# SwiGLU in a two-layer hybrid encoder trunk: gate and up products by rows, on a transposed x whose norm factor is applied behind the product

## The chip, the core and the metric

The kernel runs on one core of one Trainium2 chip. The metric is the device time of one execution in microseconds (us), lower is better. Engines: PE (TensorE, matmuls; PEld is its weight load), DVE (VectorE), ACT (ScalarE), POOL (GpSimd) and SP (SyncE, which here issues the DMAs).

## The reference

Two layers over x of 256 tokens by 1024 channels, float32. Each layer has a mixer (three groups of dilated-window attention beside a Hyena long convolution, merged by gates) and a SwiGLU, each between two RMSNorms. What the change touches is the second line of a layer's end:

```python
x = x + rms_norm(m, norm_mix_post[l])
u = rms_norm(x, norm_ffn_pre[l])                     # x * rsqrt(mean(x*x) + 1e-6) * gain
a, b = jnp.split(u @ w_gu, 2, axis=-1)               # w_gu: 1024 x 5632
x = x + rms_norm((jax.nn.silu(a) * b) @ w_down, norm_ffn_post[l])
```

## The kernel before

**Arithmetic.** A weight comes from memory as a "piece", one tile of 128 partitions by 1024 (or 768) float32. ACT rounds it to `whi` (L86, `hi_of`) and DVE, or for every fifth piece POOL, takes the rest `wlo` (L89, `lo_of`). Activations are split the same way (`UH`/`UL`). `mm3` (L80) then makes three matmuls, high by high, high by low, low by high, in place of one. All have L78 in the profile.

**Two forms of product.** `col_proj` (L409) keeps a 128x128 block of weights stationary and streams all 256 tokens, so that one piece gives 128 output channels in transposed form: 24 matmuls of 256 columns. `rows_of`/`rows` (L420, L424) keep a 128x128 block of the transposed activations stationary and stream the weights, 384 or 512 columns wide, once for each of the two tiles of 128 tokens: 12 matmuls for a piece, and the result has tokens on the partitions.

**Pieces.** `order()` (L116) lists the pieces. `split_hi` and `split_lo` take the next one; `piece()` (L171) keeps three ready ahead of the one it hands out. Raw tiles have four buffers, so SP issues the next load when an earlier raw tile has been split.

**SwiGLU before.** `ffn` (L802) takes the first 384 channels of gate and of up by rows (eight pieces of 768 columns, in `start`), multiplies SiLU(gate) by up there, and transposes the three blocks with six PE transposes (`first`, L810). The other 19 blocks are pairs of `col_proj` calls (L825), whose product (L828) is already transposed. The down product (`row_proj`, L430) takes the 22 blocks `HF`, splits each (`left`, L831) and streams 22 pieces of `w_down`.

**The passage from the mixer to the SwiGLU** is `row_proj` with `gn` 1 (the output product of the mixer): the last six pieces are first used for token tile 0 alone. While PE goes back over them for tile 1, tile 0 is normalized, added to x (`add_to_x`), normalized again (`x_rstd`, `pre_b`, with a gain tile that a DMA brings to all partitions) and turned by PE (`to_cols`, L390). Then `start` (L507) runs its eight pieces for tile 0 alone, while tile 1 goes through the same steps in `second` (L491); after six of them tile 1 is turned, and the eight pieces are run for tile 1. The order of ACT, DVE and POOL in this passage is the order of the program (`ordered`, L386); elsewhere a scheduler orders them. PE is always in program order.

**Filters.** The Hyena filters of the next layer are made by generators (`filter_chunk`, L280) that `tick()` (L98) moves on by a step, at most two of them at a time; in layer 0 five such jobs are queued at the head of `ffn`.

**PSUM.** `acc()` (L59) has eight banks.

Of the kernel before, what the change touches and what calls it, by code (L numbers as in the profile page):

```python
# [24 lines left out]
OP = mybir.AluOpType  # L25
# [15 lines left out]
PC_H, PC_G, PC_OH, PC_OA, PC_OUT, PC_GU, PC_DN = 0, 24, 40, 48, 52, 60, 98  # L41
N_PIECES = 120


def trunk(tc, nc, a, out):
# [4 lines left out]
    with es:  # L50
# [65 lines left out]
        def order():  # L116
            for l in range(DEPTH):
# [6 lines left out]
                for p in range(PC_OH, PC_GU):  # L124
# [73 lines left out]
        fpar = cst.tile([P, DEPTH, 4], F32, name="fpar")  # L198
        fc = bigt(name="fc")
# [155 lines left out]
        def rstd_of(ss):  # L355
            v, r = s1("nv"), s1("nr")
# [16 lines left out]
        def x_rstd(i):  # L373
# [3 lines left out]
            return rstd_of(ss)  # L377
# [12 lines left out]
        def to_cols(i, u, U):  # L390

            for h in range(2):
# [4 lines left out]
                hi_of(uh, t)  # L397
                lo_of(ul, t, uh)
# [31 lines left out]
        def row_proj(l, n, left, gn, nxt):  # L430


            banks = [[acc() for h in range(2)] for i in range(2)]
            g = g2 = None
# [8 lines left out]
            for k in range(n):  # L443
# [9 lines left out]
                if k == max(0, n - tail - 3):  # L453
                    g, g2 = gain(l, gn), gain(*nxt) if nxt else None
            with ordered():
# [10 lines left out]
                if nxt:  # L466
# [36 lines left out]
                S = start(U, second)  # L503
# [3 lines left out]
        def start(U, second, at=0):  # L507
# [4 lines left out]
            for n in range(START):  # L512
                pcs.append(piece(not ready))
                rows_of(U, o[n // 4][0], 0, pcs[n], n % 4, 384)
                if n == at:
                    u1 = second()
                elif n == START - 3:
                    prefetch()
                    to_cols(1, u1, U)
                if len(ready) < 2 and n < START - 1:  # L520
                    prefetch()
            for n in range(START):
                rows_of(U, o[n // 4][1], 1, pcs[n], n % 4, 384)
                done(pcs[n])
                if len(ready) < 3:
                    prefetch()
            return o
# [274 lines left out]
        def ffn(l, U, o):  # L802
            HF = [bigt(name="HF") for f in range(6)]
            hn = [sm.tile([P, 384], F32, tag="t512", bufs=7, name="hn") for i in range(2)]
            for i in range(2):
                sl = sm.tile([P, 384], F32, tag="t512", bufs=7, name="sl")
                nc.scalar.activation(sl, o[0][i][:, :384], AF.Silu)
                vtt(hn[i], o[1][i][:, :384], sl, op=OP.mult)

            def first():  # L810
                yield
                for f in range(3):
                    if f != 1:
                        t = acc()
                    for i in range(2):
                        c = (f % 2) * L + i * P
                        nc.tensor.transpose(t[:, c:c + P], hn[i][:, f * P:(f + 1) * P], ident)
                    if f:
                        w = (f % 2) * L + L
                        nc.scalar.activation(HF[0][:, (f - f % 2) * L:(f + 1) * L], t[:, :w], AF.Copy)  # L820
                yield

            queue.appendleft(first())
            for f in range(3, NF):
                oa, ob = col_proj(U), col_proj(U)  # L825
                sl = f256("silu")
                nc.scalar.activation(sl, oa, AF.Silu)
                vtt(ct(HF, f), ob, sl, op=OP.mult)  # L828
                tick()
# [164 lines left out]
```

## Time and profile before

| | us |
|---|---|
| median of three runs (1100.32 to 1102.95) | 1100.67 |
| the profiled execution, its own time | 1101.53 |
| its span, first to last instruction | 1099.8 |
| PE busy in the span | 1077.7 |
| DVE, ACT, POOL busy | 712.9, 554.0, 394.1 |

The busy time of an engine is the time in which at least one of its instructions runs. A matmul of this profile lasts longer than the distance to the next one, since they overlap; what PE can do in a time is therefore read from the starts, not from durations. The output of PE's groups by line gives the counts, the timeline gives the starts, and the chain of waits tells what the end was waiting for.

### The profile page before, as it was taken

The numbers are of one execution on the slowest core, as the hardware profiler recorded it, in microseconds if no ns is written. First come the engines' busy times: TensorE is split into PE (matmuls) and PEld (weight loads), VectorE is DVE, ScalarE is ACT, GpSimd is POOL, SyncE is SP. The second block draws the span as 40 slices with busy tenths as digits, with TensorE's granted clock in tenths as the row PEclk, the third lists the DMA queues.
The fourth block names the chain that finished last, engine by engine and source line by source line (L and its number), as shares of the span: only waits on it lengthen the run. The fifth ranks groups of instructions, "written<-read, shape, count | busy, mean of one in ns | idle before, by whom it ended". The sixth has DMA issues, their size and how long they took to land.

```text
span 1099.8 us, 18234 instructions
## 1 busy us (share of the span) xinstructions
PE 1077.7 (98%) x6984; PEld 1005.5 (91%) x6984; DVE 712.9 (65%) x1131; ACT 554.0 (50%) x828; POOL 394.1 (36%) x480
## 2 busy tenths in 40 slices
PE   8989999999999999999999999999999999999997
PEld 7989998899888899999889999998999889999986
DVE  5799986656646756665475877876445676554554
ACT  6555564443644645454465564444355455544442
POOL 2543123578713134211116714466645220111110
PEclk9999999999999999999999999999999999999999
DMA  8566544444446555656655544444455466555662
GB/s 295 177 207 196 163 140 141 151 132 128 145 163 199 185 183 185 194 179 222 198 171 172 179 148 141 133 158 150 129 158 187 164 219 191 156 189 177 206 192 77
DMA packets 60881, 189.21 MB, mean 172 GB/s; under 512 B 6903, under 2 KB 9337, under 8 KB 60794
## 3 DMA queue, kind: packets, MB, share of 16 engines
q1 hardware_dynamic: 60794, 188.04, 53.3%
q8 instruction: 55, 0.90, 0.3%
q14 instruction: 32, 0.26, 0.1%
HBM read 186.97 MB, written 1.05 MB: 171 GB/s over the span
## 4 chain that ended last, share of the span: by engine, by line
PE 88%; DVE 6%; DMA 2%; ACT 2%; issue 1%; POOL 1%; SPq 0%; DVEq 0%; POOLq 0%; ACTq 0%
PE acc L78 84%; DVE wlo L89 2%; PE acc L618 1%; DVE dl L89 1%; DMA mask<-in_mask_dram 1%; DVE dd L313 1%; ACT jk L350 1%; DMA raw<-in_wq_dram 1%; ACT whi L86 1%; PE acc L549 1%; PE acc L395 1%; PE acc L648 1%; DVE arg L239 1%; DMA w<-in_w_dram 0%; DVE X L371 0%
## 5 line engine op out<-in xcount | busy, mean ns | idle before, releaser
L86 ACT ACTIVATE whi<-raw 128x1024 fp32r<-128x1024 f32 (+1 forms) x352 | 346.3, 991 | 384.7 <-PE acc L78 292.0
L89 DVE TENSOR_TENSOR wlo<-raw,whi 128x1024 fp32r<-128x1024 f32 (+1 forms) x294 | 345.3, 1182 | 227.0 <-ACT whi L86 224.1
L78 PE MATMUL acc<-UH,whi 128*128 128x256 f32 x992 | 282.4, 285 | 0.0
L78 PE MATMUL acc<-UH,wlo 128*128 128x256 f32 x992 | 280.6, 283 | 0.0
L78 PE MATMUL acc<-UL,whi 128*128 128x256 f32 x992 | 280.6, 283 | 0.0
L89 POOL TENSOR_TENSOR wlo<-raw,whi 128x1024 fp32r<-128x1024 f32 (+1 forms) x58 | 132.9, 2292 | 405.2 <-ACT whi L86 405.1
L78 PE MATMUL acc<-whi,UH 128*128 128x384 f32 (+1 forms) x576 | 204.6, 355 | 0.0
L78 PE MATMUL acc<-wlo,UH 128*128 128x384 f32 (+1 forms) x576 | 202.0, 351 | 2.2 <-DVE wlo L89 1.4
L78 PE MATMUL acc<-whi,UL 128*128 128x384 f32 (+1 forms) x576 | 200.6, 348 | 0.0
L78 PEld LDWEIGHTS acc<-UL,whi 128*128 128x128 f32 x992 | 190.2, 192 | 0.4
L78 PEld LDWEIGHTS acc<-UH,whi 128*128 128x128 f32 x992 | 190.1, 192 | 0.4
L78 PEld LDWEIGHTS acc<-UH,wlo 128*128 128x128 f32 x992 | 190.1, 192 | 0.0
L78 PEld LDWEIGHTS acc<-wlo,UH 128*128 128x128 f32 x576 | 109.0, 189 | 9.8 <-DVE wlo L89 4.1
L78 PEld LDWEIGHTS acc<-whi,UH 128*128 128x128 f32 x576 | 109.1, 189 | 5.6 <-issue 0.7
L78 PEld LDWEIGHTS acc<-whi,UL 128*128 128x128 f32 x576 | 108.8, 189 | 5.4 <-DVE UL L89 0.2
L78 PE MATMUL acc<-whi,hs 128*128 128x512 f32 x352 | 109.0, 389 | 0.0
L78 PEld LDWEIGHTS acc<-whi,hs 128*128 128x128 f32 x352 | 66.1, 188 | 13.7
L78 PE MATMUL acc<-wlo,hs 128*128 128x512 f32 x176 | 68.5, 389 | 0.0
L828 DVE TENSOR_TENSOR HF<-acc,silu 128x256 f32<-128x256 f32 x38 | 16.1, 424 | 48.4 <-PE acc L78 48.4
L357 POOL TENSOR_SCALAR nv<-ss 128x1 f32<-128x1 f32 x16 | 7.1, 442 | 105.2 <-ACT jk L350 105.2
L78 PEld LDWEIGHTS acc<-wlo,hs 128*128 128x128 f32 x176 | 33.1, 188 | 6.7
L567 POOL TENSOR_TENSOR t<-t 128x256 f32<-128x256 f32 x32 | 36.5, 1142 | 4.3 <-DVE t L565 2.3
(168 smaller groups left out, 1570.1 us busy)
## 6 DMA issues: line engine op xcount, KB each, us to landing
raw<-in_wa_dram SPq DMA_DIRECT2D x240, 512.0 KB, 4.0
raw<-in_wq_dram SPq DMA_DIRECT2D x96, 384.0 KB, 3.5
raw<-in_wg_dram SPq DMA_DIRECT2D x16, 384.0 KB, 3.7
w<-in_w_dram SPq DMA_DIRECT2D x16, 256.0 KB, 4.2
gain<-in_gains_dram SPq DMA_DIRECT2D x7, 512.0 KB, 6.8
dec<-in_dec_dram SPq DMA_DIRECT2D x8, 256.0 KB, 3.1
bb<-in_hyb_dram SPq DMA_DIRECT2D x16, 128.0 KB, 3.3
gb<-in_bg_dram SPq DMA_DIRECT2D x8, 256.0 KB, 3.7
```

Of the source, the lines that this page charges most:

```text
L78: nc.tensor.matmul(o, lT, r, start=start, stop=stop)
L86: return nc.scalar.activation(o, i, AF.Copy)
L89: (eng or nc.vector).tensor_tensor(o, i, h, op=OP.subtract)
L239: stt(arg, k, -c, arg, op0=OP.mult, op1=OP.add)
L313: vtt(d[:, q * 256:(q + 1) * 256], h[:, q * 256:(q + 1) * 256], dec[:, e, :], op=OP.mult)
L350: nc.scalar.activation(jk, half, AF.Square, scale=D ** -0.5, accum_out=ss[:, h:h + 1])
L395: nc.tensor.transpose(t[:, q * P:(q + 1) * P], u[:, h * 512 + q * P: h * 512 + (q + 1) * P], ident)
L549: nc.tensor.transpose(t[:, q * P:(q + 1) * P], eo[:, q // 2, q % 2, :], ident)
L567: ptt(t1[:, 256:512], t2[:, 0:256], t2[:, 256:512], op=OP.add)
L618: nc.tensor.transpose(t[:, q * P:(q + 1) * P], qk[i][:, j * 384 + g * P: j * 384 + (g + 1) * P], ident)
L648: nc.tensor.transpose(t[:, q * P:(q + 1) * P], S[:, i * 512 + q * P:i * 512 + (q + 1) * P], ident)
L828: vtt(ct(HF, f), ob, sl, op=OP.mult)
```

## The change

The gate and up products of all 2816 channels are made by rows: 44 pieces of 1024 columns, each one streamed 512 wide for both token tiles. SiLU(gate) times up then has tokens on the partitions, and PE turns it, 128x128 at a time, into `HF` (`flip`), two pieces into the next chunk of 512 channels. What is turned in `to_cols` is x itself, not its norm: the gain, which now lies on the partitions (`fgain`, loaded at the head of the kernel), is multiplied in while the turned bank is split, in four quarters of 128 columns; the row factor `frs` is found after `start` and multiplied in behind the product, in SiLU's scale and in the product with up. In `start` tile 0 runs six pieces ahead of tile 1 (eight before, of 384 columns each), and the last two of the eight pieces serve both tiles at once. The filters of the next layer are queued after the first chunk has been turned. The passage from the SwiGLU to the next mixer keeps its form.

```diff
-PC_H, PC_G, PC_OH, PC_OA, PC_OUT, PC_GU, PC_DN = 0, 24, 40, 48, 52, 60, 98
-N_PIECES = 120
+PC_H, PC_G, PC_OH, PC_OA, PC_OUT, PC_DN = 0, 24, 40, 48, 52, 60
+N_PIECES = 82
+N_GU = 44
...
-                for p in range(8):
-                    yield a["wg"][l, p], 768
-                for p in range(PC_GU, N_PIECES):
+                for p in range(N_GU):
+                    yield a["wg"][l, p], 1024
+                for p in range(PC_DN, N_PIECES):
                     yield a["wa"][l, p], 1024
...
+        fgain = cst.tile([P, DEPTH, KT], F32, name="fgain")
+        frs = cst.tile([P, 2], F32, name="frs")
...
             nc.sync.dma_start(fpar, a["fpar"])
+            nc.sync.dma_start(fgain, a["fgain"])
...
-        def to_cols(i, u, U):
+        def to_cols(i, u, U, g=None):
...
                 uh, ul = (x[:, i * 512:(i + 1) * 512] for x in U[h])
-                hi_of(uh, t)
-                lo_of(ul, t, uh)
+                if g is None:
+                    hi_of(uh, t)
+                    lo_of(ul, t, uh)
+                    continue
+                parts = [(slice(q * P, (q + 1) * P), g[:, 4 * h + q:4 * h + q + 1]) for q in range(4)]
+                for w, gq in parts:
+                    nc.scalar.activation(uh[:, w], t[:, w], AF.Copy, scale=gq)
+                for w, gq in parts:
+                    stt(ul[:, w], t[:, w], gq, uh[:, w], op0=OP.mult, op1=OP.subtract)
...
+            plain = gn == 1
...
-                    g, g2 = gain(l, gn), gain(*nxt) if nxt else None
+                    g, g2 = gain(l, gn), gain(*nxt) if nxt and not plain else None
...
                 add_to_x(0, [times_gain(banks[0][h], g, h) for h in range(2)], r)
-                if nxt:
+                if plain:
+                    split_lo()
+                    split_lo()
+                    u0 = X[0]
+                elif nxt:
...
-                            to_cols(0, u0, U)
+                            to_cols(0, u0, U, fgain[:, l, :] if plain else None)
...
                     add_to_x(1, t, r)
                     split_lo()
+                    if plain:
+                        split_hi()
+                        split_lo()
+                        return X[1]
                     ss2 = new_sums()
...
-                S = start(U, second)
+                S = start(U, second, 512 if plain else 384, g=fgain[:, l, :] if plain else None)
+                if plain:
+                    for i in range(2):
+                        x_rstd(i, frs[:, i:i + 1])
...
-        def start(U, second, at=0):
+        def start(U, second, w, at=0, g=None):
...
-            for n in range(START):
+            ns = START - 2 if w == 512 else START
+            for n in range(ns):
                 pcs.append(piece(not ready))
-                rows_of(U, o[n // 4][0], 0, pcs[n], n % 4, 384)
+                rows_of(U, o[n // 4][0], 0, pcs[n], n % 4, w)
                 if n == at:
                     u1 = second()
-                elif n == START - 3:
+                elif n == ns - (2 if w == 512 else 3):
                     prefetch()
-                    to_cols(1, u1, U)
-                if len(ready) < 2 and n < START - 1:
+                    to_cols(1, u1, U, g)
+                if len(ready) < 2 and n < ns - 1:
                     prefetch()
-            for n in range(START):
-                rows_of(U, o[n // 4][1], 1, pcs[n], n % 4, 384)
+            for n in range(ns):
+                rows_of(U, o[n // 4][1], 1, pcs[n], n % 4, w)
                 done(pcs[n])
                 if len(ready) < 3:
                     prefetch()
+            for n in range(ns, START):
+                pc = piece()
+                for i in range(2):
+                    rows_of(U, o[n // 4][i], i, pc, n % 4, w)
+                done(pc)
...
-        def ffn(l, U, o):
+        def ffn(l, U, o, jobs):
...
+            def gate(oa, n):
+                hs = [sm.tile([P, 512], F32, tag="hs", bufs=5, name="hn") for i in range(2)]
+                for i in range(2):
+                    nc.scalar.activation(hs[i][:, :n], oa[i][:, :n], AF.Silu, scale=frs[:, i:i + 1])
+                return hs
+
+            def times(c, hs, ob, n):
+                for i in range(2):
+                    stt(hs[i][:, :n], ob[i], frs[:, i:i + 1], hs[i][:, :n], op0=OP.mult, op1=OP.mult)
+                held.append((c, hs, n))
+
+            def flip():
+                c, hs, n = held.pop()
+                for f in range(0, n // P, 2):
+                    t = acc()
+                    for q in range(2):
+                        for i in range(2):
+                            b = (2 * q + i) * P
+                            nc.tensor.transpose(t[:, b:b + P], hs[i][:, (f + q) * P:(f + q + 1) * P], ident)
+                    nc.scalar.activation(HF[c][:, f * L:(f + 2) * L], t, AF.Copy)
...
             def left(f):
+                if f < len(early):
+                    return early[f]
+                if f == 2:
+                    flip()
...
+            times(0, gate(o[0], 512), o[1], 512)
+            for c in range(1, 6):
+                for j in range(2 if c < 5 else 1):
+                    o = [acc() for i in range(2)]
+                    for kk in range(4):
+                        pc = piece()
+                        for i in range(2):
+                            rows_of(U, o[i], i, pc, kk, 512)
+                        done(pc)
+                        if kk % 2:
+                            tick()
+                        if held and kk == 1:
+                            flip()
+                            if c == 1:
+                                queue.extend(jobs)
+                        if c == 5 and kk > 1:
+                            early.append(left(kk - 2))
+                    if c == 5:
+                        times(c, gate(o, 256), [b[:, 256:] for b in o], 256)
+                    elif j == 0:
+                        hs = gate(o, 512)
+                    else:
+                        times(c, hs, o, 512)
...
-                queue.extend(jobs[:5])
-            U, S = ffn(l, U, S)
+            U, S = ffn(l, U, S, jobs[:5])
```

The host packs `wg` with 44 pieces of 1024 columns per layer, and `fgain` as 128 partitions by 2 layers by 8.

## Rows read from the trace of the kernel before

**Rows 1.** The page's parts 1 and 2: busy time of each engine, share of the span and instructions; and the granted TensorE clock in 40 equal slices, 9 for 90% or more.

```profile
PE 1077.7 (98%) x6984; PEld 1005.5 (91%) x6984; DVE 712.9 (65%) x1131; ACT 554.0 (50%) x828; POOL 394.1 (36%) x480
...
PEclk9999999999999999999999999999999999999999
```

**Rows 2.** The page's part 4, the chain of waits that ended last, its share of the span by engine.

```profile
PE 88%; DVE 6%; DMA 2%; ACT 2%; issue 1%; POOL 1%; SPq 0%; DVEq 0%; POOLq 0%; ACTq 0%
```

**Rows 3.** Groups of instructions by line and shape, PE, 376.7 to 565 us (the SwiGLU of layer 0 behind its passage): the first of three groups of the same size, which differ in the operands alone (high by high, high by low, low by high).

```profile
L78 PE MATMUL acc<-UH,whi 128*128 128x256 f32 x304 | 86.1, 283 | 0.0
```

**Rows 4.** The timeline of PE: start, time of one, operation. The first and the last of four runs of back-to-back matmuls: 28 of 384 columns; 24 of 512 columns; 24 of 512 columns behind transposes of another job; 52 of 256 columns.

```profile
377.30 0.34 PE L78 MATMUL acc<-whi,UH 128*128 128x384 f32 x1
...
381.98 0.33 PE L78 MATMUL acc<-whi,UH 128*128 128x384 f32 x1
...
740.11 0.40 PE L78 MATMUL acc<-whi,UH 128*128 128x512 f32 x1
...
745.35 0.39 PE L78 MATMUL acc<-whi,UL 128*128 128x512 f32 x1
...
747.28 0.48 PE L78 MATMUL acc<-whi,UH 128*128 128x512 f32 x1
...
752.59 0.39 PE L78 MATMUL acc<-whi,UL 128*128 128x512 f32 x1
...
959.80 0.28 PE L78 MATMUL acc<-UL,whi 128*128 128x256 f32 x1
...
965.92 0.28 PE L78 MATMUL acc<-UL,whi 128*128 128x256 f32 x1
```

**Rows 5.** The chain in order of time: start, us, what. Transposes by PE in the two halves of the passage of layer 0 and in the SwiGLU.

```profile
366.23 1.15 PE acc L395 x8
...
375.80 0.87 PE acc L395 x8
...
398.85 0.66 PE acc L817 x6
```

**Rows 6.** The timeline of PE in the passage of layer 0 and, last, of layer 1: start, time of one, operation, in brackets the idle time before it and what ended it.

```profile
366.15 1.23 PE L395 MATMUL acc<-ident,u 128*128 128x128 f32 x8
...
367.13 0.47 PE L78 MATMUL acc<-whi,MH 128*128 128x512 f32 x1
...
373.94 0.34 PE L78 MATMUL acc<-whi,UH 128*128 128x384 f32 x1
374.65 0.44 PE L78 MATMUL acc<-wlo,UH 128*128 128x384 f32 x1 [0.37 <-DVE wlo L89]
...
376.43 0.42 PE L78 MATMUL acc<-whi,UH 128*128 128x384 f32 x1
376.84 0.44 PE L78 MATMUL acc<-wlo,UH 128*128 128x384 f32 x1
...
910.88 0.44 PE L78 MATMUL acc<-wlo,UH 128*128 128x384 f32 x1 [0.34 <-DVE wlo L89]
```

**Rows 7.** The timeline of ACT in the passage of layer 0, merged where instructions follow each other.

```profile
371.48 0.63 ACT L350 ACTIVATE jk<-X 128x512 bf16<-128x512 f32 x1 [1.20 <-DVE X L371]
...
372.77 2.30 ACT L86 ACTIVATE whi<-raw 128x768 fp32r<-128x768 f32 x3
```

**Rows 8.** The timeline of DVE in the passage of layer 0.

```profile
370.63 1.42 DVE L371 SCALAR_TENSOR_TENSOR X<-pn,nr,X 128x512 f32<-128x512 f32 x2 [0.36 <-POOL nr L358]
...
373.63 0.96 DVE L89 TENSOR_TENSOR wlo<-raw,whi 128x768 fp32r<-128x768 f32 x1 [0.72 <-ACT whi L86]
374.51 1.41 DVE L383 SCALAR_TENSOR_TENSOR u<-X,nr,gain 128x512 f32<-128x512 f32 x2
```

**Rows 9.** Groups by line and shape, whole kernel: count, busy us, mean ns of one, idle time before them and what ended it.

```profile
L86 ACT ACTIVATE whi<-raw 128x1024 fp32r<-128x1024 f32 x240 | 253.7, 1061 | 309.9 <-PE acc L78 231.0 <-issue 67.4 <-DMA raw<-in_wa_dram 4.1
L89 DVE TENSOR_TENSOR wlo<-raw,whi 128x1024 fp32r<-128x1024 f32 x197 | 248.1, 1264 | 157.9 <-ACT whi L86 155.2 <-issue 2.0
...
L592 DVE SCALAR_TENSOR_TENSOR X<-acc,cw,X 128x192 f32<-128x192 f32 x32 | 13.2, 414 | 0.5
...
L86 ACT ACTIVATE UH<-acc 128x512 fp32r<-128x512 f32 x16 | 9.0, 597 | 10.3 <-PE acc L395 9.8 <-PE acc L78 0.5
L593 DVE SCALAR_TENSOR_TENSOR X<-acc,cw,X 128x63 f32<-128x63 f32 x32 | 8.9, 279 | 0.6
...
L332 ACT ACTIVATE ev<-acc 128x256 f32<-128x256 f32 x16 | 6.0, 378 | 4.7 <-PE acc L78 4.6
```

**Rows 10.** The timeline of SP's queue near the head: the DMA of the small filter constants `fpar`, and the next one.

```profile
11.29 0.37 SPq L212 DMA_DIRECT2D fpar<-in_fpar_dram  x1
12.27 0.35 SPq L215 DMA_DIRECT2D cw<-in_cw_dram  x1
```

**Rows 11.** The chain in order of time near the head: a DMA on it.

```profile
22.09 8.79 DMA mask<-in_mask_dram
```

**Rows 12.** Busy time of each engine (instructions in brackets) from 588 to 608 us, where the mixer of layer 1 makes filters: length, PE, PEld, DVE, ACT, POOL, clock, DMA share, GB/s.

```profile
588.00:608.00 20.00, 18.14 (x105) 17.11 (x104) 12.17 (x18) 8.58 (x15) 12.89 (x16) 1.00 0.52 159
```

**Rows 13.** The view of the tile `silu`: how long its engine (ACT or DVE) sat idle before the instructions of L827 and L828, until what, us and times.

```profile
  PE acc L78: 58.3, 38
```

**Rows 14.** The view of the tile `HF`: DVE's split of the blocks for the down product, duration least/median/most in ns, first and last start in us.

```profile
L89 DVE TENSOR_TENSOR hs<-HF,hs x44: 409/419/2475, 401.1 to 1065.0; 128x256 fp32r<-128x256 f32 x44
```

More of the change, by code (lines that the diff above doesn't have):

```diff
@@ L123, in order @@
                     yield a["wq"][l, p], 768
-                for p in range(PC_OH, PC_GU):
+                for p in range(PC_OH, PC_DN):
                     yield a["wa"][l, p], 1024
-                for p in range(8):
-                    yield a["wg"][l, p], 768
-                for p in range(PC_GU, N_PIECES):
+                for p in range(N_GU):
+                    yield a["wg"][l, p], 1024
+                for p in range(PC_DN, N_PIECES):
                     yield a["wa"][l, p], 1024
@@ L353, in new_sums, with rstd_of @@
             return sm.tile([P, 2], F32, tag="s2", bufs=4, name="ss")
-        def rstd_of(ss):
-            v, r = s1("nv"), s1("nr")
+        def rstd_of(ss, r=None):
+            v = s1("nv")
+            r = s1("nr") if r is None else r
             nc.gpsimd.tensor_scalar(v, ss[:, 0:1], ss[:, 1:2], EPS, op0=OP.add, op1=OP.add)
@@ L376, in x_rstd @@
                 square_sum(ss, h, X[i][:, HALF[h]])
-            return rstd_of(ss)
+            return rstd_of(ss, r)
         def pre_b(i, r, g):
@@ L799, in mixer @@
             return row_proj(l, KT, merged, 1, (l, 2))
-        def ffn(l, U, o):
+        def ffn(l, U, o, jobs):
             HF = [bigt(name="HF") for f in range(6)]
[L804 to L829, printed above, removed]
@@ new lines, in ffn @@
+            held = []
+            def gate(oa, n):
[7 more added lines that the diff above has]
+                held.append((c, hs, n))
@@ L831, in left @@
+            def flip():
[7 more added lines that the diff above has]
+                    nc.scalar.activation(HF[c][:, f * L:(f + 2) * L], t, AF.Copy)
+            early = []
             def left(f):
+                if f < len(early):
+                    return early[f]
+                if f == 2:
+                    flip()
@@ L854, in trunk @@
             prefetch()
-            S = start(U, lambda: pre_b(1, x_rstd(1), g), 3)
+            S = start(U, lambda: pre_b(1, x_rstd(1), g), 384, 3)
         shared[0] = True
@@ L934, in _pack @@
     d["x"] = np.ascontiguousarray(i["x"][0][PERM])
+    d["fgain"] = np.ascontiguousarray(i["norm_ffn_pre"].reshape(DEPTH, KT, P).transpose(2, 0, 1))
     d["gains"] = np.stack([i["norm_mix_pre"], i["norm_mix_post"], i["norm_ffn_pre"], i["norm_ffn_post"]], 1)
@@ L937, in _pack @@
     wq = np.empty((DEPTH, 48, P, 768), np.float32)
-    wg = np.empty((DEPTH, 8, P, 768), np.float32)
+    wg = np.empty((DEPTH, N_GU, P, 1024), np.float32)
     for l in range(DEPTH):
@@ L949, in _pack @@
         gu = i["w_gate_up"][l].reshape(D, 2, D_FF)
-        wg[l] = gu[:, :, :384].reshape(4, 2, P, 2, 384).transpose(3, 0, 2, 1, 4).reshape(8, P, 768)
-        for q in range(2):
-            wa[l, PC_GU + q:PC_DN:2] = _col_pieces(gu[:, q, 384:])
+        wg[l, :40] = gu[:, :, :2560].reshape(4, 2, P, 2, 5, 512).transpose(4, 3, 0, 2, 1, 5).reshape(40, P, 1024)
+        wg[l, 40:] = gu[:, :, 2560:].reshape(4, 2, P, 512).transpose(0, 2, 1, 3).reshape(4, P, 1024)
         wa[l, PC_DN:PC_DN + NF] = i["w_down"][l].reshape(NF, P, D)
```

2 lines of the change are left out of this document (1 added, 1 removed).

## The prediction

> **What bounds the kernel now.** I read the page's busy times first: PE is busy 98% of the span, the next engine 65%, and the granted clock is at its full level (2.4 GHz) in every slice [rows 1]. The chain of waits says the same: 88% of it is PE [rows 2]. So the time is a sum of PE work plus the few places where PE stands still, and a change is worth what it does to either. Busy time doesn't tell the first, because matmuls overlap; I took it from the distance between starts in the timeline. Then I looked for idle gaps between starts in the SwiGLU and in the passage that leads to it, and read ACT's and DVE's timelines beside them. In the SwiGLU behind the passage PE runs without gaps; in the passage it waits a few times, for a split weight and for the turned second token tile.
>
> **The distances.** 256 columns: 965.92 - 959.80 over 51 steps is 0.1200 us. 384 columns: 4.68 over 27 is 0.1733. 512 columns with activations stationary: 5.24 over 23 is 0.2278, and 5.31 over 23 = 0.2309 where transposes stand just ahead [rows 4]. From the first two, 128 columns more cost 0.0533 and a matmul has a fixed part of 0.0133 whatever its width; by that 512 columns would take 0.2266. I use 0.2278, because it is the form that the change uses, with 0.2266 and 0.2309 as bounds.
>
> The Trainium skill (TensorE: Matmul & The Clock Gate, Back-to-back issue gap) gives a fixed part of 2.5 ns, a fifth of what the rows show. By its formula, as an estimate, the wide form would save 1.3 us a layer and the 38 added transposes would take 2.1, so that PE would lose by this change. No row bears the 2.5 ns out, and the distances above decide.
>
> **Part 1: gate and up by rows.** Before, a layer has 8 pieces x 12 = 96 matmuls of 384 columns and 38 x 24 = 912 of 256, of which the 3 x 304 are seen [rows 3]: 96 x 0.1733 + 912 x 0.1200 = 16.6 + 109.4 = 126.1. After, 44 pieces x 12 = 528 of 512 columns: 528 x 0.2278 = 120.3 (119.6 to 121.9). The columns streamed are the same; the saving is the fixed part of 480 matmuls that go. Saved: 5.8 a layer (4.2 to 6.5), all of it on the path, since nothing else limits PE there.
>
> **Part 2: the transposes.** All 22 blocks are now turned for both tiles: 44 in place of 6, 38 more. Eight took 0.87 in one half of the passage and six 0.66 in the SwiGLU, 0.109 each; eight took 1.15 where PE also waited for their input, 0.144 [rows 5]. Cost: 38 x 0.109 = 4.1 a layer (to 5.5). I take 4.1: the input of `flip` is finished two pieces, 24 x 0.2278 = 5.5 us, before PE comes to it, so they should run as the unhindered ones do. The copies of the turned banks go to ACT, eleven a layer at 0.597 for a bank [rows 9], 6.6 us; ACT is busy half of the time [rows 1] and PE doesn't wait for them, as eight banks are enough: two for gate, two for up until the product is made, two for the turned blocks, two for a filter step. If that count were exceeded, PE would wait for SiLU or the product, about 1.2 to 1.5 each time.
>
> **Part 3: the passage.** Removed from tile 1's way are two square sums on ACT (371.48 to 372.77), the factor on POOL, and the scaling `u` on DVE, 1.41 [rows 7, 8]. What PE lost there: 0.54 for the low part of the sixth piece (373.94 to 374.65, less 0.17), 0.24 for the turned tile (376.43 to 376.84), 0.11 in the next two (376.84 to 377.30, less 0.35) [rows 4, 6], and 0.11 at the first tile (eight transposes over 0.98 in place of 0.87): 1.0 a layer. Layer 1 has the same wait for a low part, 0.34 by its row [rows 6].
>
> After the change: the sixth piece began at 373.94, 30 matmuls of 0.1733 behind the first, so tile 0's run starts near 368.6. Four pieces are ready then (two that `piece()` leaves, two split in the tail). A piece is six matmuls, 1.37; the fifth is needed at 374.1, the sixth at 375.4. DVE finishes x of tile 1 at 372.05 [rows 8], then splits the fifth piece until 373.3 and the sixth until 374.6 (1.26 each [rows 9]); their high parts (1.06 each) now find ACT free from about 369.4. Both are some 0.8 early. Tile 1 is turned after the fifth piece, at 375.4; x is there. The sixth piece and eight transposes cover what follows until 377.7. The split of a turned bank is dearer: quarters of 128 columns, for ACT about 0.27 (worked out from 0.378 for 256 columns and 0.597 for 512), for DVE about 0.35 (from 0.279 for 63 and 0.414 for 192) [rows 9], so 1.1 and 1.4 a bank. DVE has the seventh piece's split ahead of it until 375.9 and ends the first bank near 377.5, at the edge. That bank is what is late next. I take 1.0 recovered (0 to 1.0; a loss is a rival below).
>
> The row factor costs four square sums on ACT, 0.63 each and a read, and POOL's two small steps, after `start`'s last split; PE still has 36 matmuls of the six pieces for tile 1 and 24 of the last two to run, 13.7 us, and first needs the result in the first `flip`. Cost nothing; without that cover some 5 us once a layer.
>
> **Part 4: loads and queues.** Bytes of weights are equal (8 x 768 + 38 x 1024 against 44 x 1024 columns); in the passage the pieces are a third larger. A gain of 512 KB per layer is no longer loaded, which makes room. The filter DMAs move behind some pieces on SP, and the filter steps behind one chunk: 13 ticks are needed until the fourth chunk of filters has ended (its start at the eighth, five more steps), 17 are left in the gate and up products, so nothing slips into the next stage. At the head SP gets one more small DMA, `fgain`. No row shows it; its like, `fpar`, took 0.37 on the queue and the next followed after 0.98 [rows 10], and a later DMA of that queue is on the chain [rows 11]. Between 0 and 1.0 I take 0.4, the issue itself.
>
> **The sum.** Per layer 5.8 - 4.1 + 1.0 = 2.7 gained; two layers 5.4, less 0.4: 5.0. The profiled execution took 1101.53 (its span and 1.7 around it); 1096.5 after. It lies 0.86 over the median, so the median should be 1095.7. With all bounds at their bad end a layer loses 5.5 - 4.2 = 1.3 and the head 1.0: 1104.3; at the good end it gains 6.5 - 4.1 + 1.0 = 3.4, and the head nothing: 1093.9.
>
> **The rivals.**
> *The passage doesn't fill.* The sixteen quarters per tile pair come late, the 1.0 isn't recovered and PE waits about as much again (one bank's split, 1.4 on DVE, less the 0.4 that ACT and DVE overlap). For it: the margin at the first bank is nil. Against it: fifth and sixth piece are early, where the larger wait was. 2 x 2.0 worse: 1099.7.
> *The filters wait.* Their steps keep two ticks between stages, but a tick is now 24 x 0.2278 = 5.5 apart, not 48 x 0.1200 = 5.8, and DVE has longer instructions. Where filters press on a mixer, PE stood idle 20.00 - 18.14 = 1.9 [rows 12]. One or two such waits in layer 0: about 1098.5. Against it: PE has no such wait in the SwiGLU before.
> *The wide matmul saves nothing* (the fixed part goes with the columns): 528 x 2 x 0.1200 = 126.7, a layer loses 0.6 + 4.1 - 1.0 = 3.7, so 1100.67 + 7.4 + 0.4 = 1108.5. The 0.2278 of this form speaks against it [rows 4].
> The Trainium skill's section named above gives a result between this rival and the forecast: with a saving of 1.3 and 2.1 for transposes the median would be, as an estimate, about 1100.7.
> *The slower side: `flip` waits for DVE.* PE's order is fixed, so if the product with up isn't done when `flip` comes, PE stands. The products are two of about 0.75 on DVE (1.42 for two of this width [rows 8]); they can stand behind three splits of weights (3 x 1.26) and behind one hold of 2.0 while POOL runs (a split that takes 0.419 took 2.475 once [rows 14]): 7.3 against 5.5 of cover, 1.8 late, ten times in two layers 18: about 1113 at worst, 1106 at a mean of 1.0. It decides from a mean lateness of 0.5 a `flip` (5.0 over ten). Against it: before, SiLU and its product always sat waiting for PE, 58.3 us in 38 waits, not for each other's queue [rows 13].
>
> **How the numbers follow.** Forecast 0.67, the passage 0.14, filters 0.08, `flip` 0.08, the wide matmul 0.03. The predicted time is the forecast's, 1095.7. What a measurement of this kernel can tell from no change is about 0.3%, 3.3 us: faster is below 1097.4, slower above 1104.0. Of the forecast 0.64 lies below 1097.4, of the passage 0.04 and of the filters 0.04: faster 0.72; slower 0.09 (`flip` 0.06, the wide matmul 0.03); the rest, 0.19, is the same. The range, 1092.5 to 1100.0, takes in the good end with 1.4 for idle gaps elsewhere that may shift (filters in the mixers), the passage and the filters; left out are the last two rivals and the joint bad end.
>
> **What would show it.** In the groups by shape the 304 matmuls of 256 columns a kind and layer [rows 3] are gone and 176 of 512 columns stand in their place; their starts lie 0.228 apart, not 0.240. Transposes of the product rise from 6 to 44 a layer and take 0.11 each; a gap ahead of them that DVE ends is the `flip` rival. In the passage no idle time of PE is ended by DVE's `wlo`, and one of up to 0.2 by `UL`. I would be wrong if PE's steps in the SwiGLU are wider than 0.231, if the first turned bank costs over 1 us, or if the head moves by more than 1.

## The result and the profile after

| | before | after |
|---|---|---|
| median, us | 1101.45 (1100.32 to 1102.95, 4 runs) | 1096.11 (1095.02 to 1096.78, 4 runs) |
| the profiled execution, us | 1101.53 | 1096.27 |
| its span, us | 1099.8 | 1094.5 |

The ratio is 0.9943 (95%: 0.9927 to 0.9959), which is 4.5 to 8.0 us with its middle at 6.3; the medians differ by 5.3. The prediction was 1095.7, with 5.0 gained.

The page of the changed kernel, parts 1, 2 and 4, against [rows 1, 2]:

```profile
PE 1073.5 (98%) x6100; PEld 960.3 (88%) x6100; DVE 704.3 (64%) x1126; ACT 565.5 (52%) x848; POOL 395.5 (36%) x479
...
PEclk9989999999999999999999999999999999999999
...
PE 88%; DVE 5%; DMA 3%; POOL 1%; ACT 1%; issue 1%; SPq 0%; DVEq 0%; POOLq 0%; ACTq 0%
```

PE is still the bound. 884 instructions of PE are gone (960 matmuls less, 76 transposes more), and it is as full as before. The 8 in the row of the clock is a stretch in mixer 0, taken up at the end. Groups by shape, changed kernel, PE, 376.7 to 565 us (the SwiGLU of layer 0 behind its passage), against [rows 3]:

```profile
L79 PE MATMUL acc<-whi,UH 128*128 128x512 f32 x164 | 64.3, 392 | 0.0
...
L855 PE MATMUL acc<-ident,hn 128*128 128x128 f32 x44 | 5.8, 272 | 0.0
```

The first row is one of three kinds (the others have 165): they stand for the 304 of 256 columns. It is 176 a kind in the layer, and the window begins behind the first of them. The second row is the 44 transposes. The starts give their price. Timeline of PE, first and last of 37 matmuls of 512 columns in layer 1; then two pieces of the chain in order of time (start, us, what), eight transposes of x in the passage (L400) and eight of the product (`flip`, L855):

```profile
931.97 0.40 PE L79 MATMUL acc<-whi,UL 128*128 128x512 f32 x1
...
940.14 0.39 PE L79 MATMUL acc<-whi,UL 128*128 128x512 f32 x1
```

```profile
374.86 0.87 PE acc L400 x8
...
396.20 0.87 PE acc L855 x8
```

36 steps in 8.17 us are 0.2269 each; a transpose takes 0.109. The view of line L855 names nothing that PE waited for ahead of a `flip` (the list under "sat idle" is empty):

```profile
L855 PE MATMUL acc<-ident,hn x88: 270/272/273, 396.0 to 1033.4; 128*128 128x128 f32 x88
its engine sat idle before it (us, times) until:
```

To see where the time went, I took from both timelines of PE the start of the first matmul that reads a stage's operand, `UH` of a SwiGLU, `hs` of a down product, `UH` of the next mixer, and subtracted neighbours:

| stage | starts before | starts after | length before | after | difference |
|---|---|---|---|---|---|
| head, mixer 0 and its output product | (0) | (0) | 368.60 | 367.45 | -1.15 |
| gate and up, layer 0 | 368.60 | 367.45 | 138.06 | 135.00 | -3.06 |
| down, layer 0 | 506.66 | 502.45 | 61.02 | 62.49 | +1.47 |
| mixer 1 and its output product | 567.68 | 564.94 | 337.16 | 337.58 | +0.42 |
| gate and up, layer 1 | 904.84 | 902.52 | 128.64 | 125.07 | -3.57 |
| down, layer 1, to the last matmul | 1033.48 | 1027.59 | 59.64 | 60.10 | +0.46 |
| last matmul starts | 1093.12 | 1087.69 | | | -5.43 |

Four of the 44 transposes (`left`, at the third block) are now part of a down product: 4 x 0.109 = 0.44, which is layer 1's 0.46. In layer 1 the whole length of gate and up is accounted for: 528 x 0.2269 for the matmuls and 48 x 0.109 for the transposes (40 of the product, 8 of the second token tile) make 125.0, and 125.07 were measured. Layer 0's down product has 1.0 more than its 0.44. Its cause is in the timeline: first PE, then ACT, changed kernel.

```profile
550.32 0.61 PE L79 MATMUL acc<-whi,hs 128*128 128x512 f32 x2
551.59 0.50 PE L79 MATMUL acc<-wlo,hs 128*128 128x512 f32 x1 [0.66 <-DVE wlo L90]
```

```profile
545.28 2.01 ACT L87 ACTIVATE whi<-raw 128x1024 fp32r<-128x1024 f32 x2 [2.99 <-DMA raw<-in_wa_dram]
548.08 2.01 ACT L87 ACTIVATE whi<-raw 128x1024 fp32r<-128x1024 f32 x2 [0.79 <-DMA raw<-in_wa_dram]
```

Two matmuls from 550.32 should end in a start at 550.77; the next is at 551.59, 0.82 late, waiting for a low part. Ahead of that ACT waited for the piece itself, which came 0.79 after ACT was free. The kernel before has no such wait of PE there.

The passage of layer 0 after the change: PE, then ACT and DVE, then POOL, against [rows 6 to 8]:

```profile
372.89 0.39 PE L79 MATMUL acc<-whi,UH 128*128 128x512 f32 x1
373.44 0.50 PE L79 MATMUL acc<-wlo,UH 128*128 128x512 f32 x1 [0.16 <-DVE wlo L90]
373.77 0.39 PE L79 MATMUL acc<-whi,UL 128*128 128x512 f32 x1
...
374.70 1.03 PE L400 MATMUL acc<-ident,X 128*128 128x128 f32 x8
375.49 0.48 PE L79 MATMUL acc<-whi,UH 128*128 128x512 f32 x1
375.81 0.40 PE L79 MATMUL acc<-wlo,UH 128*128 128x512 f32 x1
...
377.43 0.40 PE L79 MATMUL acc<-whi,UL 128*128 128x512 f32 x1
```

```profile
389.76 0.69 ACT L840 ACTIVATE hn<-acc,frs 128x512 f32<-128x512 f32 x1
```

```profile
367.06 2.16 DVE L410 SCALAR_TENSOR_TENSOR UL<-acc,fgain,UH 128x128 fp32r<-128x128 f32 x8 [2.42 <-ACT UH L408]
...
369.73 1.98 DVE L376 SCALAR_TENSOR_TENSOR X<-pn,nr,X 128x512 f32<-128x512 f32 x2
371.63 5.10 DVE L90 TENSOR_TENSOR wlo<-raw,whi 128x1024 fp32r<-128x1024 f32 x3
376.65 1.11 DVE L410 SCALAR_TENSOR_TENSOR UL<-acc,fgain,UH 128x128 fp32r<-128x128 f32 x4
```

```profile
370.42 0.74 POOL L298 TENSOR_TENSOR sd<-w 128x256 f32<-128x256 f32 x1 [0.73 <-DMA w<-in_w_dram]
371.12 1.19 POOL L302 TENSOR_TENSOR sd<-w 128x256 f32<-128x256 f32 x1
372.26 1.71 POOL L298 TENSOR_TENSOR sd<-w 128x256 f32<-128x256 f32 x1
...
387.98 0.56 POOL L363 TENSOR_TENSOR frs<-nv,mh 128x1 f32<-128x1 f32 x1
```

Three readings. PE's waits are 0.32 (373.44 - 372.89 less a step) and 0.11 for one low part, that of the fifth piece, and none for x or a turned bank; the first step behind transposes is 0.32, 0.09 more than a step, and is part of their 0.109 each. The row factor is there at 388.54, SiLU reads it at 389.76. And POOL's filter additions, which the program queues later than before, stand in the middle of the passage: `w` landed early and POOL took them up. DVE is longer beside them: X x2 1.98 against 1.42 [rows 8], three splits 5.10 against 3 x 1.26 = 3.8 [rows 9]. In layer 1, which makes no filters, the passage has no wait at all.

### The profile page after: what moved, and what is told of

Its sections match the earlier page's. It is cut to its first block, busy times and chain, and to the rows that moved or that the text cites. A ratio compares the mean times of both kernels' runs of the same rounds, so it can differ in the third digit from the quotient of the medians.

```text
span 1094.5 us, 16421 instructions
## 1 busy us (share of the span) xinstructions
PE 1073.5 (98%) x6100; PEld 960.3 (88%) x6100; DVE 704.3 (64%) x1126; ACT 565.5 (52%) x848; POOL 395.5 (36%) x479
## 4 chain that ended last, share of the span: by engine, by line
PE 88%; DVE 5%; DMA 3%; POOL 1%; ACT 1%; issue 1%; SPq 0%; DVEq 0%; POOLq 0%; ACTq 0%
PE acc L79 84%; DMA raw<-in_wq_dram 2%; DVE wlo L90 1%; PE acc L648 1%; PE acc L855 1%; DMA mask<-in_mask_dram 1%; DVE dd L317 1%; PE acc L579 1%; PE acc L678 1%; ACT whi L87 1%; DVE dl L90 1%; DVE arg L243 1%; PE acc L400 0%; DMA raw<-in_wa_dram 0%; POOL t L597 0%
## 5 line engine op out<-in xcount | busy, mean ns | idle before, releaser
L79 PE MATMUL acc<-whi,UH 128*128 128x512 f32 (+1 forms) x864 | 321.5, 372 | 0.0
L79 PE MATMUL acc<-wlo,UH 128*128 128x512 f32 (+1 forms) x864 | 317.3, 367 | 2.4 <-POOL wlo L90 1.6
L79 PE MATMUL acc<-whi,UL 128*128 128x512 f32 (+1 forms) x864 | 316.9, 367 | 0.1
L79 PEld LDWEIGHTS acc<-wlo,UH 128*128 128x128 f32 x864 | 163.4, 189 | 22.0 <-DVE wlo L90 2.3
L79 PE MATMUL acc<-UH,whi 128*128 128x256 f32 x384 | 110.3, 287 | 0.0
L79 PE MATMUL acc<-UH,wlo 128*128 128x256 f32 x384 | 108.6, 283 | 0.0
L79 PE MATMUL acc<-UL,whi 128*128 128x256 f32 x384 | 108.6, 283 | 0.0
L79 PEld LDWEIGHTS acc<-UL,whi 128*128 128x128 f32 x384 | 73.6, 192 | 0.3
L79 PEld LDWEIGHTS acc<-UH,whi 128*128 128x128 f32 x384 | 73.5, 192 | 0.2
L79 PEld LDWEIGHTS acc<-UH,wlo 128*128 128x128 f32 x384 | 73.5, 191 | 0.0
```

The lines of the kernel that those rows point to most:

```text
L79: nc.tensor.matmul(o, lT, r, start=start, stop=stop)
```

## The experiments

Each is an edit of the changed kernel unless it says otherwise. Ratios are against the kernel before in the same series; the changed kernel stands at 0.9943. 0.001 is 1.1 us.

**half_wide**: is the gain the fixed part of a matmul?

```diff
+        def halves(U, o, i, pc, kk):
+            for s in (0, 256):
+                for k in range(2):
+                    kt = 2 * kk + k
+                    w = slice(k * 512 + s, k * 512 + s + 256)
+                    mm3(o[:, s:s + 256], *u_cols(U, kt, i), pc[0][:, w], pc[1][:, w], kt == 0 and s == 0, kt == KT - 1 and s > 0)
...
-                            rows_of(U, o[i], i, pc, kk, 512)
+                            halves(U, o[i], i, pc, kk)
```

> The changed kernel, but each 512-wide matmul of the gate and up products behind the passage (36 pieces a layer, 432 matmuls) is made as two of 256 columns into the same bank. My theory, a fixed part of 0.0133 us for every matmul whatever its width: 432 more a layer x 0.0133 = 5.8, two layers 11.5, so about 1107.6 against the changed kernel's 1096.1, with starts 0.120 apart. Rival, the time goes with the columns and the gain of the change came from elsewhere: no difference, 1096.1, starts 0.114 apart.

1105.85, ratio 1.0043 (1.0021 to 1.0065): 1.0% slower than the change, 11 us, for 864 matmuls more, 0.0127 each. Gate and up of layer 1 take 130.65 (125.07 in the change): 5.58 / 432 = 0.0129. Ten steps of its timeline:

```profile
931.90 0.28 PE L79 MATMUL acc<-whi,UH 128*128 128x256 f32 x1
...
933.10 0.28 PE L79 MATMUL acc<-wlo,UH 128*128 128x256 f32 x1
```

0.1200 a step, two of them 0.2400 against 0.2269. The fixed part, put at 0.0133, came out at 0.0127 to 0.0131 in these three ways.

**turn_twice**: what does a transpose cost?

```diff
-                    for q in range(2):
+                    for q in (0, 1, 0, 1):
```

> The changed kernel with every transpose of the product made twice into the same place, 44 more a layer. My theory, 0.109 us each and all of it on the path: 44 x 0.109 x 2 = 9.6, so 1105.7. Rival one, transposes wait for their input and cost 0.144: 12.7, 1108.8. Rival two, they fall into time in which PE waits anyway: 1096.1.

1104.47, ratio 1.0024 (1.001 to 1.0037): 0.81% over the change, 8.9 us for 88 transposes, 0.10 each. The chain has one `flip` of sixteen:

```profile
395.11 1.75 PE acc L855 x16
```

1.75 / 16 = 0.109. They are paid in full.

**passage_alone**: the kernel before with the turned x (the change's `to_cols`, `plain` branches and `fgain`), without the product by rows. It leaves the row factor out.

```diff
+            plain = gn == 1
...
-                S = start(U, second)
+                S = start(U, second, g=fgain[:, l, :] if plain else None)
```

> The kernel before with the changed passage alone: x is turned without its norm, the gain multiplied in by quarters, the fgain load at the head; gate and up stay as before. The row factor of the norm before SwiGLU is left out altogether, since the transposed form has no place for it. My theory, 1.0 a layer gained, 0.4 lost at the head: 1.6 below the kernel before. Rival, the passage is worth nothing: within 0.5 of the kernel before or above it.

1099.72, ratio 0.9983 (0.997 to 0.9996): 1.9 us gained. By the landmarks of the table each layer's gate and up get 0.6 shorter (137.45 and 128.02) and each output product 0.28: 0.9 a layer, about what the waits of [rows 6] promised.

**normed_passage**: the change without that part, so x is normalized before it is turned, as in the kernel before; tile 0 still runs six pieces ahead.

```diff
-            plain = gn == 1
+            plain, w = False, 512 if gn == 1 else 384
...
-                S = start(U, second, 512 if plain else 384, g=fgain[:, l, :] if plain else None)
+                S = start(U, second, w, g=fgain[:, l, :] if plain else None)
...
-                    nc.scalar.activation(hs[i][:, :n], oa[i][:, :n], AF.Silu, scale=frs[:, i:i + 1])
+                    nc.scalar.activation(hs[i][:, :n], oa[i][:, :n], AF.Silu)
...
-                    stt(hs[i][:, :n], ob[i], frs[:, i:i + 1], hs[i][:, :n], op0=OP.mult, op1=OP.mult)
+                    vtt(hs[i][:, :n], ob[i][:, :n], hs[i][:, :n], op=OP.mult)
```

> The changed kernel with the passage's norm put back: x is normalized and scaled before it is turned, the banks are split whole, and no row factor stands behind the product; six pieces ahead and all products by rows stay. My theory, the shorter way of tile 1 was worth 1.0 a layer: 1098.1, and up to 1100 if the longer way now ends behind the six pieces; PE again waits for wlo or for the turned tile in both layers. Rival, the passage is worth nothing and the whole gain lies in the matmuls: 1096.1.

1100.78, ratio 0.999 (0.9977 to 1.0004): 0.47% over the change, 5.2 us. Timeline of PE in layer 0's passage, and the windows over it (columns as in [rows 12]; the clock is third from the end):

```profile
377.17 0.68 PE L400 MATMUL acc<-ident,u 128*128 128x128 f32 x4 [1.93 <-DVE u L388]
378.31 1.11 PE L400 MATMUL acc<-ident,u 128*128 128x128 f32 x4 [0.46 <-DVE u L388]
```

```profile
370.00:377.60 7.60, 5.67 (x28) 4.42 (x26) 6.34 (x6) 5.86 (x10) 6.33 (x7) 1.00 0.41 119
377.60:381.20 3.60, 3.14 (x12) 2.50 (x10) 3.60 (x4) 2.85 (x5) 3.60 (x3) 0.53 0.22 84
```

With the norm on tile 1's way six pieces don't cover it. In layer 0 PE waits 1.93 and 0.46 for `u`, and behind that the granted clock stands at its half level (1.2 GHz) for nearly all of 377.6 to 381.2. Layer 0 loses 0.7 in the output product and 3.7 in gate and up. Layer 1, which makes no filters, loses 0.8 and 0.7, with a wait of 0.38 for the turned tile and no fall of the clock. So the two parts seem to hold each other up: by the ratios they give 1.9 (passage_alone) and 1.1 (this run) alone, 6.3 together. The three intervals leave some 2.7 of doubt about the 3.3 between (an estimate from their widths), so the size of it is not fixed by these runs.

**eight_ahead**: tile 0 runs all eight pieces before tile 1.

```diff
-            ns = START - 2 if w == 512 else START
+            ns = START
-                elif n == ns - (2 if w == 512 else 3):
+                elif n == ns - (4 if w == 512 else 3):
```

> The changed kernel with eight 512-wide pieces ahead for tile 0 in place of six (tile 1 is still turned behind the fifth). My theory, the eighth piece is needed at the pace of six matmuls, 1.37, while DVE also splits the turned tile: a wait of 0.3 to 1.0 a layer for its low part, 0.6 to 2 above the changed kernel. Rival, how far tile 0 runs ahead is indifferent as soon as the turned tile is covered: no difference.

1101.33, ratio 0.9989 (0.9976 to 1.0003): 5 us slower than the change. PE in layer 0's passage, what ACT and DVE do there, and the window behind the waits:

```profile
379.96 0.51 PE L79 MATMUL acc<-whi,UH 128*128 128x512 f32 x1 [1.44 <-ACT whi L87]
381.31 0.71 PE L79 MATMUL acc<-wlo,UH 128*128 128x512 f32 x1 [0.84 <-DVE wlo L90]
```

```profile
378.84 3.91 ACT L87 ACTIVATE whi<-raw 128x1024 fp32r<-128x1024 f32 x4
```

```profile
380.04 4.62 DVE L90 TENSOR_TENSOR wlo<-raw,whi 128x1024 fp32r<-128x1024 f32 x4
```

```profile
381.40:384.90 3.50, 3.50 (x9) 2.76 (x10) 3.26 (x3) 3.50 (x9) 0.77 (x1) 0.51 0.40 118
```

The eighth piece comes late: ACT begins its high part at 378.84 and DVE its low part at 380.04, each straight behind the quarters of the turned tile. Again two waits (starts 378.14, 379.96 and 381.31: 1.6 and 1.1) are followed by a stretch at half level, in which a matmul of 512 columns takes 0.427 (381.81 to 384.37, six steps) and not 0.227; eight of them make 1.6 us more. Layer 1 has the same two waits, shorter (1.4 in all); its gate and up lose 1.4 (126.51), and the clock stays at its full level.

**pool_later**: POOL's filter additions made to wait for `frs`, by a copy of it into their output, in the first chunk.

```diff
+            if l == 1 and cc == 0:
+                nc.gpsimd.tensor_copy(sd[:, 0:1], frs[:, 1:2])
             h = ptt(sd[:, 0:256], w[:, 0:256], w[:, 256:512], op=OP.add)
```

> The changed kernel; the two POOL adds with which each of the first two filter jobs in layer 0 begins are made to follow the second row factor (a one-column copy of it into their tile), so that POOL no longer does them in the passage. My theory, POOL's adds held DVE there (x of tile 1 in 1.98 in place of 1.42, three splits in 5.10 in place of 3.8), and PE's wait of 0.32 + 0.11 for a low part in layer 0 comes from that: the wait is gone as in layer 1, 0.4 below the changed kernel, which stands at 0.9943 of the kernel before. Rival, DVE is late by its own work: the wait stays, no difference.

1096.64, ratio 0.9946 (0.9929 to 0.9963): no gain. In the passage DVE is freed, since only one addition is left beside it, and PE doesn't wait:

```profile
373.99 4.04 DVE L90 TENSOR_TENSOR wlo<-raw,whi 128x1024 fp32r<-128x1024 f32 x3
```

4.04 in place of 5.10. But the wait is 0.43 us, below what the medians can tell, and it is also gone in runs without this edit (after_again, below). So this run doesn't show what the wait came from.

**filters_at_head**: the jobs queued ahead of the first chunk. **fgain_late**: the small DMA behind those of the head.

```diff
             times(0, gate(o[0], 512), o[1], 512)
+            queue.extend(jobs)
...
-                            if c == 1:
-                                queue.extend(jobs)
```

```diff
-            nc.sync.dma_start(fgain, a["fgain"])
...
             hi_of(mask[:, :, :].rearrange("p a b -> p (a b)"), t)
+            nc.sync.dma_start(fgain, a["fgain"])
```

> The changed kernel with the filters of the next layer queued ahead of the first chunk, as before the change. My theory, the place in the queue hardly matters, because their loads and POOL steps start early either way: within 1 of the changed kernel. Rival, the place behind the first chunk was needed: PE waits of 1 to 2 like the 1.9 of the mixer, so 1 to 3 above it.

> The changed kernel with the small fgain load behind the constants of the mixer on SP, and not ahead of them. My theory, it cost 0.4 at the head (0 to 1.0): the first filter matmul comes 0.4 to 0.6 earlier after the start than the changed kernel's 60.21, and the time is 0.4 lower. Rival, the head is not moved by one small load: no difference.

1096.91, ratio 0.9948 (0.9932 to 0.9964), and 1095.36, 0.9946 (0.9929 to 0.9963). Neither place matters: the filter load `w` is issued at 365.07 in filters_at_head and at 364.92 in the change; the first filter matmul starts at 59.60 before, 60.21 in the change, 59.76 with the late DMA, and between 58.8 and 60.5 in all other kernels that load `fgain` at the head.

**after_again, pool_phase, head_and_phase**: the changed kernel once more; the share of splits that go to POOL moved by two in layer 0's down product (in the 35 us ahead of the late piece POOL starts one, in the kernel before two); and both moves together with filters_at_head.

```diff
-                share = shared[0] and count[1] % POOL_LO == 0 or count[1] == 6
+                turn = count[1] + (2 if 152 < count[1] < 175 else 0)
+                share = shared[0] and turn % POOL_LO == 0 or count[1] == 6
```

> The changed kernel once more, unaltered, beside the next two on one chip: 0.9943 of the kernel before, 0.993 to 0.996. In the down product of layer 0 PE should again wait 0.8 for a low part, and the mixers' idle gaps should differ from the first profile's, if they are chance.

> The changed kernel with the count that gives every fifth split to POOL shifted by two pieces in the down product of layer 0, so that it falls as in the kernel before (which had 46 pieces ahead of it, not 44). My theory, the wait for a low part near 550 us (0.82 + 0.11), which the kernel before didn't have, comes from the missing POOL split shortly ahead of the stretch in which pieces are used at twice the pace: the wait is gone and the layer's down product takes 61.5 in place of 62.5; 0.9 below the changed kernel. Rival, the weights land late (ACT waits for the DMA there): the wait stays, no difference.

> The shift of the count and the filters queued ahead of the first chunk, both together. My theory, both waits of layer 0 that are left are gone (0.4 in the passage, 0.9 in the down product): 1.4 below the changed kernel, 0.993 of the kernel before. Rival, the wait for a low part stays as in the rival of the run with the shift alone: 0.4 below or none.

1095.73, ratio 0.9945 (0.9929 to 0.9961); 1095.53, 0.9943 (0.993 to 0.9956); 1096.77, 0.9953 (0.9938 to 0.9968). The wait in the down product stays in all three, in pool_phase:

```profile
551.99 0.51 PE L79 MATMUL acc<-wlo,hs 128*128 128x512 f32 x1 [0.45 <-DVE wlo L90]
```

So the missing split on POOL isn't its cause; that theory falls. What is left is that the pieces land late (ACT's waits for the DMA, shown above). Before, ACT waited there too, 2.42 and 0.29, and PE did not. SP's queue shows the load that ACT waits for, before and after; ACT's line is from the kernel before:

```profile
547.31 0.33 SPq L140 DMA_DIRECT2D raw<-in_wa_dram  x1
```

```profile
543.57 0.33 SPq L141 DMA_DIRECT2D raw<-in_wa_dram  x1
```

```profile
550.75 2.02 ACT L86 ACTIVATE whi<-raw 128x1024 fp32r<-128x1024 f32 x2 [0.29 <-DMA raw<-in_wa_dram]
```

The load isn't issued later: 40.65 behind the first matmul of the stage before, 41.12 after, where 0.44 of PE's time went to transposes. It takes longer, 3.4 until ACT starts (3.5 in passage_alone) against 4.5 in the change and 4.1 to 4.5 in the other kernels by rows. Why a load of the same size takes longer there is open.

after_again settles another wait: the passage of layer 0, in which PE has no wait this time. DVE and POOL there:

```profile
372.13 1.41 DVE L376 SCALAR_TENSOR_TENSOR X<-pn,nr,X 128x512 f32<-128x512 f32 x2
373.46 5.12 DVE L90 TENSOR_TENSOR wlo<-raw,whi 128x1024 fp32r<-128x1024 f32 x3
```

```profile
372.84 1.30 POOL L298 TENSOR_TENSOR sd<-w 128x256 f32<-128x256 f32 x1 [0.75 <-DMA w<-in_w_dram]
```

POOL's addition starts 0.71 behind DVE's pair here, 0.69 in the execution shown above, and either POOL (0.74, then X takes 1.98) or DVE (1.41, then POOL takes 1.30) goes through unhindered. The wait of PE is there in the three profiles where POOL won (1.89 to 1.98 for X: 0.24 to 0.32 of wait) and in none of the five others with the same passage, where DVE did (1.41 or 1.42). The three splits take 5.12 here too, so their length alone doesn't make the wait; x of tile 1, 0.57 later, does on top of it. That is read from executions that differ by chance, not by an edit made for it.

No kernel tried here beats the changed one by more than the scatter.

## Why the prediction was right

By its own terms, in us, both layers together:

| term | predicted | measured | from |
|---|---|---|---|
| gate and up by rows | -11.6 | -12.6 | 528 x 0.2269 = 119.8 against 126.1, twice |
| transposes | +8.2 | +8.3 | 76 x 0.109; turn_twice |
| passage | -2.0 | -1.1 and -0.6 | layer 1, layer 0: what is left of the stages |
| down product of layer 0 | 0 | +0.9 | 0.82 and 0.11 in PE's starts |
| `fgain` at the head | +0.4 | not seen | fgain_late |
| sum | -5.0 | -5.1 | the table of stages, without head and mixers |

- **Gate and up.** Right in mechanism and size. The step came out at 0.2269, between 0.2266 and the 0.2278 that I took. That the fixed part goes with each matmul is shown by half_wide; the rival "the wide matmul saves nothing" falls. Each matmul here has a weight load of its own (6100 of either on the page), so the runs don't tell to which of the two the part belongs. The Trainium skill (TensorE: Matmul & The Clock Gate, Back-to-back issue gap) gives 2.5 ns for this part in its formula of the isolated gap, from which the prediction estimated 1100.7; the runs show 13 ns, in the steps and in half_wide, and the measurement decides.
- **Transposes.** Right: 0.109 each, and `flip` never waited. The product is done at 392.8, the transposes begin at 396.0; POOL's holds reach DVE in other places. That rival falls.
- **Passage.** Right for layer 1: -3.57 - 0.16 (its output product) + 0.46 = -3.27 is -6.3 + 4.1 - 1.1. In layer 0 one wait came back. The step that failed there is the timing of the fifth piece's low part. It was put 4.7 behind the start of tile 0's run (373.3 for a start near 368.6), 0.8 early; it ended at 5.93 (373.38 for 367.45), 0.3 late. x of tile 1 was ready at 4.26 and not at 3.45, and the split took 1.75 and not 1.26. Of the 0.81 for x, 0.25 stand in the profiles without the wait as well; the rest came where POOL's addition went first. The split takes 1.75 to 1.77 with the wait and without, with POOL's additions beside it both times. The fear for the first turned bank was wrong too. Quarters on DVE follow each other at 0.27, not 0.35, and PE reads the bank quarter by quarter: it uses the first `UL` at 377.43, while the bank is finished at 377.76.
- **Loads and queues.** The step "the filters move behind some pieces on SP" failed: their place in the program doesn't set when they run. `w` was issued at 383.69 before and at 364.92 after, though it is queued later, and at 365.07 where filters_at_head queues it early. Mixer 1 shows no press of filters (273.9 before up to its first matmul on `zh`, 274.3 after, 272.8 to 275.0 over the other kernels), so the rival of waiting filters isn't borne out.
- **Not foreseen.** The late piece in layer 0's down product, 0.9, present in every kernel by rows (0.4 to 0.8 for its first part), and neither before nor in passage_alone.
- **Luck.** Head and mixers moved by -0.3 in sum, but single stages of unchanged work by up to 1.5 (mixer 0 from its first filter matmul to its first on `zh`: 245.6 before, 244.1 after, 246.8 in after_again, the same program). The pair of DVE at 103 us, in the last section, has the largest part in that. One profile can't place a term of 0.4; only the medians of a series and a stage without such waits (layer 1's SwiGLU) can. That the sum of the terms, -5.1, lies so near the forecast is in part luck: the passage gave 0.3 less than its term and the down product 0.9 of loss that no term had, against 1.0 more from the matmuls and 0.4 at the head that was not seen.

What I undervalued is how the parts hang together. normed_passage and eight_ahead each cost 5 us, more than the terms gave, since a wait of PE isn't paid with its length alone: in layer 0 of eight_ahead 2.7 of waits and 1.6 of slower clock make 4.3, and its gate and up lose 4.0 to 4.5 (139.0 against 135.0 in the change and 134.5 in after_again). In layer 1 of the same run, where the clock held, 1.4 of waits cost 1.4.

## What to carry to other kernels

Where PE is the bound and already full, count its instructions: here each matmul cost 13 ns beside its columns, so a form with about half as many (528 for 1008) was worth 6.3 us a layer, and the price of transposes that come with it (0.109 each) can be read from the same trace beforehand. Judge a lead such as "six pieces ahead" together with what it has to cover, since waits of 2.7 us here cost 4.3 where the clock fell behind them, and waits of 1.4 cost no more than their length where it didn't. Look for work that a scheduler may pull into a tight passage, on engines that the change doesn't speak of.

## What the runs showed of the hardware

**DVE and POOL hold each other up by whole instructions.** The first place is the passage above, where POOL's additions alternate with DVE's splits (0.74 alone, 1.71 beside them). The kernel before has it in mixer 0, DVE and POOL:

```profile
102.81 3.49 DVE L89 TENSOR_TENSOR dl<-dd,dh 128x512 fp32r<-128x512 f32 x2
```

```profile
103.13 2.63 POOL L89 TENSOR_TENSOR wlo<-raw,whi 128x1024 fp32r<-128x1024 f32 x1 [12.64 <-ACT whi L86]
```

POOL ends at 105.76, and DVE's second split ends 0.54 after that, at 106.30, though the first took 0.68 or less. The same pair took 1.28 in the changed kernel (103.71), where POOL started at 104.52, behind it. The Trainium skill (SBUF — State Buffer, Who interferes with whom) states that a VectorE instruction with two SBUF inputs contends with a GpSimd instruction that reads SBUF, and that the ports they share are an exclusive lock; these rows agree.

Which way it goes differs between executions of one program: of the thirteen profiles seven have the long pair, after_again among them (3.46), and six the short one, the change among them. The windows over it, the change and after_again (PE is the first busy time, DVE the third):

```profile
100.00:113.00 13.00, 13.00 (x105) 12.74 (x104) 12.96 (x34) 8.96 (x14) 5.36 (x3) 1.00 0.62 189
```

```profile
100.00:113.00 13.00, 9.89 (x77) 9.31 (x76) 13.00 (x28) 7.52 (x12) 4.95 (x4) 1.00 0.64 196
```

DVE is busy throughout in both, and where its pair is long PE stands still for 3.1 of the 13.0.

**The clock falls behind PE's waits, and not always at the same ones.** Windows near 65 us before and after, then near 303 us in after_again, where the one near 65 us stayed at full level:

```profile
63.50:67.00 3.50, 3.48 (x14) 3.48 (x15) 3.50 (x7) 0.42 (x2) 3.50 (x7) 0.51 1.00 332
```

```profile
62.80:69.80 7.00, 5.67 (x21) 5.67 (x22) 6.19 (x11) 2.36 (x5) 6.68 (x12) 0.51 0.82 274
```

```profile
301.20:304.70 3.50, 3.50 (x15) 3.50 (x13) 1.29 (x2) 1.09 (x2) 0.00 (x0) 0.51 0.70 236
```

Each follows a stretch in which PE stood still for part of the time (55.0 to 63.5 before: busy 5.50 of 8.50; 298.0 to 301.2 in after_again: 0.82 of 3.20). Two executions of one program, the change and after_again, had it in different places. By the starts of the same matmuls it cost the change 2.5 near 65 us and after_again 1.6 near 303, so it doesn't explain why after_again's mixer 0 is the longer one by 2.7: that one falls behind by 3.6 between 106 and 113 us, with the long pair of DVE.
